# Hand-listed events around three layer norms: the turns that a front does not read go behind the second half's sums

## Chip, cores, metric

The kernel runs on one NeuronCore of a Trainium2 chip. The metric is the device time of one execution in microseconds, the median of several runs. Beside it stands one profiled execution, with times of every instruction.

## What is computed

The reference is one decoder layer on 256 tokens of width 2048, in float32:

```python
h = layer_norm(alpha * h + 0.5 * swiglu(h, w_ffn1_gu, w_ffn1_down))          # norm 0
rq, rk, rv, rg, aq, ak, av, gate_r, gate_a = split(h @ w_in)
mixed = (sigmoid(gate_r) * ret_branch + sigmoid(gate_a) * att_branch) @ w_mix_out
h = layer_norm(alpha * h + mixed)                                            # norm 1
h = layer_norm(alpha * h + 0.5 * swiglu(h, w_ffn2_gu, w_ffn2_down))          # norm 2
ple = sigmoid(h @ w_ple_gate) * (p @ w_ple_proj)
h = layer_norm(alpha * h + ple)                                              # norm 3
```

`swiglu` has an inner width of 5632; `ret_branch` is a chunkwise retention with eight heads, `att_branch` a sliding-window attention with sixteen. The change touches what stands around norms 0, 1 and 2, in the text called the first, the second and the third norm.

## The kernel before

**Weights.** Weights come in chunks of 512 KB. SP issues the loads (line 105, tiles `r...`), ACT makes the high part of each chunk (line 91, tiles `h...`), the DVE the low part (line 92, tiles `l...`), and PE multiplies three times for each product: low by high, high by high, high by low (lines 291 to 293). A list `plan` holds the chunks in the order of use. `fill` takes from it: it loads a chunk while there is room and the queued work is under a limit `far`, and makes a loaded one while the made work is under a limit `ahead` and `room["quiet"]` is not set. `take` hands the next made chunk to the matmuls, `done` gives its slots back and calls `fill`. All instructions are written in one order (the scheduler is told to keep it), so each engine runs its own in that order, and an instruction that waits holds up those behind it on its engine.

**The tokens.** The 256 tokens are two halves of 128 rows, t=0 and t=1. A row half has sixteen blocks of 128 columns. A norm needs the whole row, and the matmuls behind it need the rows turned: features in partitions. So around each norm stand:

- *The held-out steps* (`held_out`): the last chunks before the norm. Their products for t=0 come first, then those for t=1, so that the norm of t=0 runs beside the second half of these matmuls.
- *Sums* (`Norm.normal(t)`): the last block of columns is added to the rows on the DVE (line 891, in the mixers 1280), its statistics are taken (line 530), the reciprocal root of the variance is computed in small DVE instructions, and the first four column blocks are normed (lines 501 and 502).
- *Turns* (`Norm.turn(t, c)`, c = 0 to 3), each four column blocks: the DVE norms the rows of the next turn (`more`), PE transposes (line 509, tile `lnps`; for c=0 two pairs, otherwise four at once), ACT and DVE make high and low part of the result (`ht`, lines 91 and 92). In the second norm ACT also copies two turns into tiles `keep`.
- *The blocks put by* (`put_by`; first and second norm): products of the embedding input `pt` with a small weight, 12 matmuls for each of two blocks, into banks `pp`. ACT copies them to `pps` behind all other events of that stretch, and SP stores them.
- *The front* (`Norm.first`): the first six steps behind the norm (a step is six matmuls of one chunk with one row half), first all six for t=0, then all six for t=1. They read column blocks 0 to 11 in the first and the third norm, thus turns c = 0 to 2; in the second norm 0 to 5, thus turns c = 0 and 1. After the front the steps go on with all columns.

In the held-out stretch n counts half steps of t=1 and on through the blocks put by; in the front n counts steps, 1 to 6 for t=0 and 7 to 12 for t=1. A tuple of such n says when the next event of a fixed list comes:

```python
at, self.at = self.at, self.at + 1
if at == 4:
    self.normal(1)
else:
    self.turn(at // 5, at % 5)
if at == 8:
    quiet(False)
```

So the events are always (0,0), (0,1), (0,2), (0,3), the sums of t=1, (1,0), (1,1), (1,2), (1,3), and behind the last of them making of chunks is allowed again ("go"). It is forbidden (`quiet(j >= len(steps) - 2)`) from the last two held-out steps of t=0 on.

For the three norms these are the places: the first norm has (8, 10, 11, 12, 12) in the held-out stretch and (4, 6, 7, 8) in the front; the second has the same; the third has (8, 11) and then (1, 3, 3, 6, 7, 9, 10).

Of the kernel before, what the change touches and what calls it, by code (L numbers as in the profile page):

```python
# [48 lines left out]
def layer(ctx: ExitStack, tc: tile.TileContext, io):  # L49
# [134 lines left out]
    def fill(must=False):  # L184

        while True:
            queued = sum(u.time for u in ready)
            left = room["slots"] - room["used"]
            wanted = must and not ready or not room["quiet"] and queued < room["ahead"]
            if loaded and wanted and loaded[0].makes <= left:  # L190
                u = loaded.pop(0)
                u.make()
                room["used"] += u.keeps - u.loads
                ready.append(u)
                continue
            first = loaded[0] if loaded else plan[0] if plan else None
            queued += sum(u.time for u in loaded)
            if plan and queued < room["far"] and plan[0].loads + first.makes <= left:
                u = plan.pop(0)
                u.load()  # L200
                room["used"] += u.loads
                loaded.append(u)
                continue
            return

    def take(key):
        if not ready:
# [12 lines left out]
    def quiet(on):  # L220
        room["quiet"] = on
# [197 lines left out]
            done(u)  # L419
            run_side()  # L420

    def held_out(steps, lhs, sums, of_columns, first_done, between, calm=True):

        kept = []
        for j, (key, k0, n) in enumerate(steps):
            u = take(key)
            kept.append(u)
            tokens_chunk(u.chunk, k0, lhs, [sums[t][n] for t in range(2)], (0,))  # L430
            if calm:
                room["ahead"] -= u.time
                room["far"] -= u.time
                quiet(j >= len(steps) - 2)
            fill()
            run_side()
            of_columns(0, j)
        first_done()
        for j, (key, k0, n) in enumerate(steps):
            for kk in range(2):  # L440
                tokens_chunk(kept[j].chunk, k0, lhs, [sums[t][n] for t in range(2)], (1,), (kk,))
                between(2 * j + kk + 1)
            done(kept[j])
            of_columns(1, j)
# [72 lines left out]
    class Norm:  # L517
# [32 lines left out]
            else:  # L550
                ln_turn(*args, 4 * c, 4, self.keep.get(c))

        def follow(self, n, times):


            while times and times[0] == n:
                times.pop(0)
                at, self.at = self.at, self.at + 1
                if at == 4:
                    self.normal(1)  # L560
                else:
                    self.turn(at // 5, at % 5)
                if at == 8:
                    quiet(False)

        def run(self, steps, lhs, times, blks=()):


            self.vectors = vectors.pop()
            self.new = big.tile([P, KD, 512], F32R, tag="ht", name=f"ht{self.i}")  # L570
            per = len(steps) // len(self.cols)
            self.at, times = 0, list(times)
# [5 lines left out]
            held_out(steps, lhs, self.sums, of_columns, lambda: self.normal(0), lambda n: self.follow(n, times))  # L578
            if blks:
                put_by(blks, lambda n: self.follow(2 * len(steps) + n, times))  # L580
            assert not times
# [6 lines left out]
        def first(self, steps, lhs, sums, times):  # L588


            kept, times = [], list(times)
            for j, (key, k0, n) in enumerate(steps):
                u = take(key)
                kept.append(u)
                tokens_chunk(u.chunk, k0, lhs, [sums[t][n] for t in range(2)], (0,))
                fill()
                self.follow(j + 1, times)
            for j, (key, k0, n) in enumerate(steps):
                tokens_chunk(kept[j].chunk, k0, lhs, [sums[t][n] for t in range(2)], (1,))
                done(kept[j])  # L600
                self.follow(len(steps) + j + 1, times)
            assert self.at == 9
            self.put_away()

    def block_stats(stats, y, col):
# [140 lines left out]
    def ffn(name, i, ht, norm, keep, residual, keepers, away):  # L746
# [28 lines left out]
        for j in range(KF // 4):  # L775
            pg, pu = banks(f"{name}g{j}"), banks(f"{name}u{j}")
            units = gu_units(j)
            plain = len(units) - sum(kind == "S" for kind, p in units)
            n_of = {(0, 0): KD, (0, 1): KD, (1, 0): KD, (1, 1): KD}
            for kind, p in units:  # L780
                if kind == "S":
                    for at in ((0, 0), (0, 1), (1, 0)):
                        n_of[at] -= 1
                    n_of[1, 1] -= 2
            sums = [[Sum((pg, pu)[n][t], n_of[t, n]) for n in range(2)] for t in range(2)]
            got = []

            if norm is not None and j == 0:
                front, units = units[:FRONT_PAIRS], units[FRONT_PAIRS:]
                steps = [(gu_keys(name, 0)(n, p), 2 * p, n) for _, p in front for n in range(2)]  # L790
                norm.first(steps, rhs, sums, (4, 6, 7, 8))
                slots_for_weights(24)

            def before(u, j=j, offset=KD // 2 - len(units)):
                u += offset
                if j == 0 and norm is None and u % 2 == 0:
                    first_chunk(u // 2)
                    if u == 6:
# [12 lines left out]
            if got:  # L811
                g, v = got
                for x, ps in ((g, pg), (v, pu)):
                    for t in range(2):
                        dve.tensor_tensor(x[:, t], x[:, t], ps[t], ALU.add)  # L815
                act.activation(g, g, AF.Silu)  # L816
                dve.tensor_tensor(v, g, v, ALU.mult)
            else:
                v = slot([P, 2, 512], F32, f"{name}v{j}")
                for t in range(2):  # L820
                    act.activation(v[:, t], pg[t], AF.Silu)
                for t in range(2):
                    dve.tensor_tensor(v[:, t], v[:, t], pu[t], ALU.mult)
            later(2, lambda j=j, v=v: turned(j, v))
# [50 lines left out]
        def before_unit(u):  # L875
# [4 lines left out]
                load_for_norm(i)  # L880
            if u == len(second) - 1:
                make_for_norm()

        pt_ = [banks(f"{name}e{t}") for t in range(2)]
        sums = [[Sum(pt_[t][n], n_of[1][t, n]) for n in range(2)] for t in range(2)]
# [5 lines left out]
            dve.tensor_tensor(sl, sl, p, ALU.add)  # L891

        norm = Norm((2, 3), sums, combine, y, stats, i, 4 * LN_EPS, keepers, away)
        norm.run(steps, lhs, *(((8, 10, 11, 12, 12), (0, 1)) if i < 2 else ((8, 11),)))
        return norm


# [53 lines left out]
    def mixers(ht, norm, residual, keepers, away):  # L951
# [17 lines left out]

        ps = banks("rv0")  # L970
        sums = [[Sum(ps[t], KD)] for t in range(2)]
        norm.first([(("w_rv", 0, c), 2 * c, 0) for c in range(FRONT)], rhs, sums, (4, 6, 7, 8))
        slots_for_weights(24)
        for c in range(FRONT, KD // 2):
            u = take(("w_rv", 0, c))
# [327 lines left out]
            run_side()  # L1303
        steps = [(("w_mix", 3, c), 2 * c, 0) for c in range(first, KD // 2)]
        norm = Norm((3,), sums, combine, y, stats, 1, LN_EPS, keepers, away)
        norm.run(steps, lhs, (8, 10, 11, 12, 12), (2, 3))
        return norm


    def embedding(ht, norm, y):  # L1310
# [17 lines left out]
        for blk in range(4):  # L1328
# [4 lines left out]
            if blk == 0:  # L1333
                for j in range(4):
                    pp[j] = load_columns(pp, j, "ppr")
                steps = [(key + (c,), 2 * c, 0) for c in range(FRONT)]
                norm.first(steps, lhs, [[s] for s in sums], (1, 3, 3, 6, 7, 9, 10))
                slots_for_weights(24)
                for c in range(FRONT, KD // 2):
                    u = take(key + (c,))  # L1340
# [20 lines left out]
            held_out(steps, lhs, [[s] for s in sums], lambda t, j: None, first_done, lambda n: None, False)  # L1361
            finish(3, pgs[1], sg, 1)
            last_norm(1, *ln_stats(stats[:, 1], 3, 1, LN_EPS))

# [146 lines left out]
```

## Time and profile before

| | |
|---|---|
| time, median of 3 runs | 2303.19 us (2302.16 to 2305.45) |
| the profiled execution: its own time, its span | 2305.66 us, 2303.6 us |
| busy: PE, DVE, ACT | 99%, 84%, 51% of the span |
| PE busy from 400 to 800 us (first norm near 710) | 394.24 of 400 us |
| PE busy from 1200 to 1600 us (second norm near 1490) | 398.48 of 400 us |
| PE busy from 2000 to 2303 us (third norm near 2200, and the end) | 286.01 of 303 us |

Busy time of PE comes from modelled ends of matmuls that overlap: a matmul of 512 columns is shown with some 0.39 us, but the next starts sooner. So the text counts from start to start. An idle time in brackets counts from the shown end of the instruction before.

In a row of the timeline stand the start in us from the span's start, the duration, the engine, the line, the operation, the tile written and the tile read, and in brackets the idle time ahead of it with what ended it. "x2" means that two such instructions were merged. A row of the windows gives from:to, the length, busy time with count for PE, PEld (weight loads), DVE, ACT and POOL, then the granted clock of PE, the DMA share and GB/s.

### The profile page before, as it was taken

What the parts mean: (1) busy time and instruction counts of PE and PEld (TensorE: products, weight loads), DVE (VectorE), ACT (ScalarE), POOL (GpSimd) and SP (SyncE); (2) the same over time, 40 slices, a digit from 0 to 9 for tenths busy, and PEclk for the clock granted to TensorE, in tenths of its full rate; (3) what the DMA queues carried; (4) which work ended last, traced back from release to release, by engine and by line L of the source; (5) the groups of instructions that cost most, each with busy time, mean ns of one, the idle gap of its engine ahead of it and who ended that gap; (6) DMA issues with size and microseconds to landing.
All of it is one profiled execution on the core that took longest, in us unless ns stands there. A gap on an engine that the chain in (4) does not pass through costs nothing.

```text
span 2303.6 us, 28759 instructions
## 1 busy us (share of the span) xinstructions
PE 2271.7 (99%) x10466; PEld 1882.5 (82%) x10466; DVE 1945.0 (84%) x2467; ACT 1184.4 (51%) x1427; POOL 96.0 (4%) x53
## 2 busy tenths in 40 slices
PE   9999999999999999999999999999999999999997
PEld 7788888888887888888778888888888888888876
DVE  7999999988988774677789786779999999889876
ACT  5555555555553342435566454355565565655432
POOL 0000000000000430124000000000000000000000
PEclk9999999999999999999999999999999999999999
DMA  9566666665576665555447567576556566565771
GB/s 317 164 219 192 192 206 195 201 207 182 214 279 237 202 215 169 171 161 163 139 156 236 170 224 274 171 245 206 197 191 203 183 209 215 170 220 193 289 256 56
DMA packets 193725, 465.70 MB, mean 202 GB/s; under 512 B 14768, under 2 KB 16048, under 8 KB 193584
## 3 DMA queue, kind: packets, MB, share of 16 engines
q1 hardware_dynamic: 191456, 460.91, 60.8%
q10 hardware_dynamic: 2128, 2.97, 0.4%
q8 instruction: 82, 1.34, 0.2%
q14 instruction: 59, 0.48, 0.1%
HBM read 455.43 MB, written 8.39 MB: 201 GB/s over the span
## 4 chain that ended last, share of the span: by engine, by line
PE 95%; DVE 3%; DMA 1%; issue 0%; ACT 0%; SPq 0%; ACTq 0%; DVEq 0%
PE f2g L293 3%; PE f2g L291 3%; PE f2g L292 3%; PE f1g L291 3%; PE f1g L292 3%; PE f1g L293 3%; PE rqk L242 3%; PE f2u L292 2%; PE f2u L291 2%; PE f2u L293 2%; PE f1u L291 2%; PE f1u L293 2%; PE f1u L292 2%; PE aqk L242 2%; PE f2d L291 2%; PE f1d L291 2%
## 5 line engine op out<-in xcount | busy, mean ns | idle before, releaser
L92 DVE TENSOR_TENSOR lf_gu<-rf_gu,hf_gu 128x1024 fp32r<-128x1024 f32 (+1 forms) x283 | 334.2, 1213 | 9.6 <-ACT hf_gu L91 9.1
L91 ACT CAST hf_gu<-rf_gu 128x1024 fp32r<-128x1024 f32 (+1 forms) x283 | 282.1, 1045 | 19.4 <-DMA rf_gu<-in_f_gu 19.4
L92 DVE TENSOR_TENSOR lw_in_f<-rw_in_f,hw_in_f 128x1024 fp32r<-128x1024 f32 x140 | 195.6, 1427 | 29.3 <-ACT hw_in_f L91 27.1
L92 DVE TENSOR_TENSOR lf_down<-rf_down,hf_down 128x1024 fp32r<-128x1024 f32 x152 | 180.9, 1219 | 27.5 <-ACT hf_down L91 22.0
L91 ACT CAST hf_down<-rf_down 128x1024 fp32r<-128x1024 f32 x152 | 155.3, 1051 | 77.0 <-DMA rf_down<-in_f_down 27.0
L91 ACT CAST huf_gu<-uf_gu 128x1024 fp32r<-128x1024 f32 x70 | 73.7, 1053 | 159.2 <-DVE uf_gu L164 153.5
L91 ACT CAST hw_in_f<-rw_in_f 128x1024 fp32r<-128x1024 f32 x140 | 138.9, 1051 | 2.3 <-DMA rw_in_f<-in_w_in_f 2.0
L291 PE MATMUL f1g<-hf_gu,xt 128*128 128x512 f32 x247 | 97.2, 393 | 5.4 <-ACT hf_gu L91 5.4
L293 PE MATMUL f1g<-lf_gu,xt 128*128 128x512 f32 x247 | 96.8, 392 | 0.0
L292 PE MATMUL f1g<-hf_gu,xt 128*128 128x512 f32 x247 | 96.8, 392 | 0.0
L291 PE MATMUL f2g<-hf_gu,ht 128*128 128x512 f32 x247 | 96.5, 391 | 0.0
L293 PE MATMUL f2g<-lf_gu,ht 128*128 128x512 f32 x247 | 96.2, 389 | 0.0
L292 PE MATMUL f2g<-hf_gu,ht 128*128 128x512 f32 x247 | 96.1, 389 | 0.0
L91 ACT CAST hvf_gu<-vf_gu 128x1024 fp32r<-128x1024 f32 x70 | 73.8, 1054 | 29.4 <-DVE vf_gu L166 29.4
L816 ACT ACTIVATE eve<-eve 128x1024 f32<-128x1024 f32 x20 | 21.2, 1062 | 127.2 <-DVE eve L815 127.2
L92 DVE TENSOR_TENSOR luf_gu<-uf_gu,huf_gu 128x1024 fp32r<-128x1024 f32 x70 | 85.2, 1218 | 0.0
L92 DVE TENSOR_TENSOR lvf_gu<-vf_gu,hvf_gu 128x1024 fp32r<-128x1024 f32 x70 | 85.2, 1217 | 0.0
L291 PE MATMUL f2u<-hf_gu,ht 128*128 128x512 f32 x212 | 83.5, 394 | 0.0
L291 PE MATMUL f1u<-hf_gu,xt 128*128 128x512 f32 x212 | 83.3, 393 | 0.0
L292 PE MATMUL f2u<-hf_gu,ht 128*128 128x512 f32 x212 | 82.5, 389 | 0.0
L293 PE MATMUL f2u<-lf_gu,ht 128*128 128x512 f32 x212 | 82.5, 389 | 0.0
L292 PE MATMUL f1u<-hf_gu,xt 128*128 128x512 f32 x212 | 82.5, 389 | 0.0
(1333 smaller groups left out, 6433.7 us busy)
## 6 DMA issues: line engine op xcount, KB each, us to landing
rf_gu<-in_f_gu SPq DMA_DIRECT2D x351, 512.0 KB, 5.0
rf_down<-in_f_down SPq DMA_DIRECT2D x176, 512.0 KB, 4.5
rw_in_f<-in_w_in_f SPq DMA_DIRECT2D x148, 512.0 KB, 4.4
rw_rv<-in_w_rv SPq DMA_DIRECT2D x32, 512.0 KB, 4.6
rw_ret<-in_w_ret SPq DMA_DIRECT2D x32, 512.0 KB, 4.7
rw_mix<-in_w_mix SPq DMA_DIRECT2D x32, 512.0 KB, 4.3
rw_pg<-in_w_pg SPq DMA_DIRECT2D x32, 512.0 KB, 4.7
rw_att<-in_w_att SPq DMA_DIRECT2D x16, 512.0 KB, 5.3
```

Of the source, the lines that this page charges most:

```text
L91: act.copy(dst_hi, src)
L92: (lo_engine or dve).tensor_tensor(dst_lo, src, dst_hi, ALU.subtract)
L242: pe.matmul(ps[f], hi[:, kk, f * P : (f + 1) * P], rhs(k), start=k == 0, stop=k == n_k - 1,)
L291: pe.matmul(o, al, bh, start=first, stop=False)
L292: pe.matmul(o, ah, bh, start=False, stop=False)
L293: pe.matmul(o, ah, bl, start=False, stop=self.left == 0)
L816: act.activation(g, g, AF.Silu)
```

## The change

Each norm now gets a written list of events, each with its place n and with what happens: a turn (t, c), "sums" (the sums of t=1), "make" (one more chunk is made, whatever `quiet` says) or "go" (making is allowed again).

- First norm: making is forbidden sooner, from the last unit ahead of the held-out steps on, and `held_out` gets calm=4, so all four of its first-half steps are quiet. With that the fifth and sixth chunk of the front (`rv_4`, `rv_5`) are not made ahead of the sums of t=0 but by two events "make" behind turn (0,2), ahead of the sums of t=1. Turn (0,3) goes from the end of the held-out stretch into the front, behind turn (1,2).
- Second norm: turns (0,2) and (0,3) go into the front, (0,2) between (1,1) and (1,2), (0,3) between (1,2) and (1,3); the sums of t=1 come behind (0,1). (1,0) comes at n=3 and not 4.
- Third norm: turn (0,3) goes from n=3 to n=8, between (1,1) and (1,2); the sums of t=1 come at n=1 and not at n=3.
- "go" comes at n=10 in all three; in the first two norms it was at n=8, in the third at n=10.

Every engine issues the same instructions as before; SP's list has the same order too.

```diff
+    def make_next():
+        u = loaded.pop(0)
+        assert u.makes <= room["slots"] - room["used"]
+        u.make()
+        room["used"] += u.keeps - u.loads
+        ready.append(u)
...
-    def held_out(steps, lhs, sums, of_columns, first_done, between, calm=True):
+    def held_out(steps, lhs, sums, of_columns, first_done, between, calm=2):
...
-                quiet(j >= len(steps) - 2)
+                quiet(j >= len(steps) - calm)
...
-        def follow(self, n, times):
-            while times and times[0] == n:
-                times.pop(0)
-                at, self.at = self.at, self.at + 1
-                if at == 4:
+        def follow(self, n, events):
+            while events and events[0][0] == n:
+                what = events.pop(0)[1]
+                if what == "sums":
                     self.normal(1)
+                elif what == "make":
+                    make_next()
+                elif what == "go":
+                    quiet(False)
                 else:
-                    self.turn(at // 5, at % 5)
-                if at == 8:
-                    quiet(False)
+                    self.turned.append(what)
+                    self.turn(*what)
...
@@ ffn: the front of the second norm
-                norm.first(steps, rhs, sums, (4, 6, 7, 8))
+                norm.first(steps, rhs, sums, (
+                    (3, (1, 0)), (5, (1, 1)), (7, (0, 2)), (8, (1, 2)), (9, (0, 3)), (10, (1, 3)), (10, "go"),
+                ))
...
@@ ffn: ahead of the held-out steps
             if u == len(second) - 1:
                 make_for_norm()
+                quiet(i < 2)
...
@@ ffn: the held-out stretch of the first (i < 2) and the third norm
-        norm.run(steps, lhs, *(((8, 10, 11, 12, 12), (0, 1)) if i < 2 else ((8, 11),)))
+        if i < 2:
+            events = ((8, (0, 0)), (10, (0, 1)), (11, (0, 2)), (12, "make"), (12, "make"), (12, "sums"))
+            norm.run(steps, lhs, events, (0, 1), 4)
+        else:
+            norm.run(steps, lhs, ((8, (0, 0)), (11, (0, 1))))
...
@@ mixers: the front of the first norm
-        norm.first([(("w_rv", 0, c), 2 * c, 0) for c in range(FRONT)], rhs, sums, (4, 6, 7, 8))
+        norm.first([(("w_rv", 0, c), 2 * c, 0) for c in range(FRONT)], rhs, sums, (
+            (5, (1, 0)), (6, (1, 1)), (8, (1, 2)), (9, (0, 3)), (10, (1, 3)), (10, "go"),
+        ))
...
@@ mixers: the held-out stretch of the second norm
-        norm.run(steps, lhs, (8, 10, 11, 12, 12), (2, 3))
+        norm.run(steps, lhs, ((8, (0, 0)), (10, (0, 1)), (10, "sums")), (2, 3))
...
@@ embedding: the front of the third norm
-                norm.first(steps, lhs, [[s] for s in sums], (1, 3, 3, 6, 7, 9, 10))
+                norm.first(steps, lhs, [[s] for s in sums], (
+                    (1, (0, 2)), (1, "sums"), (6, (1, 0)), (7, (1, 1)), (8, (0, 3)), (9, (1, 2)),
+                    (10, (1, 3)), (10, "go"),
+                ))
```

More of the change, by code (lines that the diff above doesn't have):

```diff
@@ L551, in turn, with run @@
                 ln_turn(*args, 4 * c, 4, self.keep.get(c))
-        def follow(self, n, times):
-            while times and times[0] == n:
-                times.pop(0)
-                at, self.at = self.at, self.at + 1
-                if at == 4:
+        def follow(self, n, events):
+            while events and events[0][0] == n:
+                what = events.pop(0)[1]
+                if what == "sums":
                     self.normal(1)
-                else:
-                    self.turn(at // 5, at % 5)
-                if at == 8:
-                    quiet(False)
-        def run(self, steps, lhs, times, blks=()):
+                elif what == "make":
+                    make_next()
+                elif what == "go":
+                    quiet(False)
+                else:
+                    self.turned.append(what)
+                    self.turn(*what)
+        def run(self, steps, lhs, events, blks=(), calm=2):
             self.vectors = vectors.pop()
@@ L571, in run @@
             per = len(steps) // len(self.cols)
-            self.at, times = 0, list(times)
+            self.turned, events = [], list(events)
             def of_columns(t, j):
@@ L576, in of_columns @@
                     self.columns(t, j // per)
-            held_out(steps, lhs, self.sums, of_columns, lambda: self.normal(0), lambda n: self.follow(n, times))
+            held_out(steps, lhs, self.sums, of_columns, lambda: self.normal(0), lambda n: self.follow(n, events), calm)
             if blks:
-                put_by(blks, lambda n: self.follow(2 * len(steps) + n, times))
-            assert not times
+                put_by(blks, lambda n: self.follow(2 * len(steps) + n, events))
+            assert not events
         def put_away(self):
@@ L586, in put_away, with first @@
                     sync.dma_start(self.away[c], self.y[c])
-        def first(self, steps, lhs, sums, times):
-            kept, times = [], list(times)
+        def first(self, steps, lhs, sums, events):
+            kept, events = [], list(events)
             for j, (key, k0, n) in enumerate(steps):
@@ L596, in first @@
                 fill()
-                self.follow(j + 1, times)
+                self.follow(j + 1, events)
             for j, (key, k0, n) in enumerate(steps):
@@ L600, in first @@
                 done(kept[j])
-                self.follow(len(steps) + j + 1, times)
-            assert self.at == 9
+                self.follow(len(steps) + j + 1, events)
+            assert not events and len(set(self.turned)) == 8
             self.put_away()
@@ L1360, in embedding @@
             steps = [(key + (c,), 2 * c, 0) for c in range(KD // 2)]
-            held_out(steps, lhs, [[s] for s in sums], lambda t, j: None, first_done, lambda n: None, False)
+            held_out(steps, lhs, [[s] for s in sums], lambda t, j: None, first_done, lambda n: None, 0)
             finish(3, pgs[1], sg, 1)
```

## The prediction

> **What bounds the kernel now.** I read the page first, then the waits of PE, then the timeline of PE, DVE and SP around the three norms, and the granted clock in short windows there.
>
> ```profile
> PE 2271.7 (99%) x10466; PEld 1882.5 (82%) x10466; DVE 1945.0 (84%) x2467; ACT 1184.4 (51%) x1427; POOL 96.0 (4%) x53
> ```
> PE is busy for all but 32 us of the span of 2303.6 us. The change adds and removes no instruction, so only what PE loses between matmuls can be won. The waits of PE (total, times, longest) say where:
>
> ```profile
> PE lnps L509 <- DVE f1y L502: 5.3, 3, 4.8
> PE lnps L509 <- DVE f2y L502: 2.4, 3, 1.6
> PE lnps L509 <- DVE mixy L502: 1.2, 3, 0.5
> ```
> Apart from the start, the end and some single microseconds, PE waits at the turns (the transposes, `lnps`) of the three norms, and for the DVE, which makes the rows that PE turns. The first norm carries the longest wait. PE there, start and duration first:
>
> ```profile
> 706.00 0.39 PE L293 MATMUL f1e<-lf_down,f1ah 128*128 128x512 f32 x1
> 711.15 0.66 PE L509 MATMUL lnps<-ident,f1y 128*128 128x128 f32 x2 [4.77 <-DVE f1y L502]
> 711.98 0.69 PE L509 MATMUL lnps<-ident,f1y 128*128 128x128 f32 x2 [0.17 <-DVE f1y L502]
> ...
> 728.01 0.41 PE L509 MATMUL lnps<-ident,f1y 128*128 128x128 f32 x2 [0.51 <-ACT ht L91]
> ...
> 732.83 0.60 PE L509 MATMUL lnps<-ident,f1y 128*128 128x128 f32 x4
> ...
> 734.66 0.60 PE L509 MATMUL lnps<-ident,f1y 128*128 128x128 f32 x4
> ...
> 740.57 0.39 PE L291 MATMUL rv<-hw_rv,ht 128*128 128x512 f32 x1
> ```
> At 706.00 PE starts its last matmul of the second sums (the second row half, t=1); the next event is the first transpose at 711.15. The idle also has a tail:
>
> ```profile
> 710.00:715.00 5.00, 3.68 (x10) 2.76 (x11) 4.86 (x11) 0.75 (x2) 0.00 (x0) 0.50 0.03 13
> ```
> The granted clock (the column after POOL) is 0.50 just after the gap. So the gap costs its 4.77 us and some slow matmuls. Two units are read from these rows. A turn and a step of six matmuls together take 734.66 - 732.83 = 1.83 us; from 734.66 a turn and four steps take 740.57 - 734.66 = 5.91 us; so a **step is 1.36 us** and a **turn 0.47 us**. 740.57 is the first matmul behind the front, the mark by which I count this norm.
>
> Why the DVE is late is in its own timeline:
>
> ```profile
> 699.43 0.68 DVE L92 TENSOR_TENSOR pt<-praw,pt 128x512 fp32r<-128x512 f32 x1
> 702.85 2.53 DVE L92 TENSOR_TENSOR lw_rv<-rw_rv,hw_rv 128x1024 fp32r<-128x1024 f32 x2 [2.73 <-ACT hw_rv L91]
> 705.30 0.68 DVE L891 TENSOR_TENSOR f1y<-f1y,f1e 128x512 f32<-128x512 f32 x1
> ...
> 711.44 0.48 DVE L502 SCALAR_TENSOR_TENSOR f1y<-f1y,rstd,ln_b 128x256 f32<-128x256 f32 x1
> ...
> 713.93 0.75 DVE L502 SCALAR_TENSOR_TENSOR f1y<-f1y,rstd,ln_b 128x512 f32<-128x512 f32 x1
> 714.60 0.75 DVE L92 TENSOR_TENSOR ht<-lnps,ht 128x256 fp32r<-128x256 f32 x2
> ...
> 722.55 0.68 DVE L891 TENSOR_TENSOR f1y<-f1y,f1e 128x512 f32<-128x512 f32 x1
> ...
> 736.86 2.36 DVE L92 TENSOR_TENSOR lw_rv<-rw_rv,hw_rv 128x1024 fp32r<-128x1024 f32 x2 [0.26 <-ACT hw_rv L91]
> ```
> The split of `pt` ends at 700.1. Then the DVE stands 2.73 us, waiting for ACT casts of two weight chunks, splits them (702.85), and only at 705.30 adds the first sums to the rows. These sums were there earlier: the 24 matmuls of the second half precede 706.23, so the first half ended at about 706.23 - 4 x 1.36 = 700.8, its first column block 2.7 us before.
>
> **First norm, part by part.** The two chunk splits go behind the turns (0,0) to (0,2), so the DVE adds the first sums at 700.1 instead of 705.30, 5.2 us sooner; the second block is wanted 1.3 us later, when it is there. PE's transposes of (0,0) at 711.15 and 711.98 could start at 705.95 and 706.8. PE is free at 706.23: the first does not wait, the second waits 0.4 us. Then follow 24 matmuls (5.44 us) and the turns (0,1) and (0,2) without (0,3), 0.94 us; with 0.2 for the pair itself the front starts at 706.8 + 6.6 = 713.4. The rows for (0,1), ready at 714.68 before (713.93 + 0.75), come at 709.5 and are wanted at 709.7: covered, barely. No gap of 4.8 us is left, so the half clock goes too.
>
> What is late next is the second norm, because the two chunk splits stand ahead of its sums. From 709.5 the DVE has the two small splits of the first turn (714.60, 0.75 together), four row operations of 0.75, two splits of the shape of `pt`'s, 0.68 each, and the two chunk splits, 2.53 together: 7.6 us by durations, 7.1 start to start (2.53 from 702.85 overlaps the next start at 705.30 by 0.08, as do its neighbours). The second sums are added at 716.6 instead of 722.55. Behind them only this norm's own work waits. The second transposes of (1,0) move by the same 5.95 us from 728.01 to 722.06. PE comes there at 713.4 + 5 steps = 720.2 and loses about 1.5 us in two pieces. Then seven steps and four turns ((1,1), (1,2), (0,3), (1,3)) are left: 0.2 + 9.52 + 1.88 = 11.6, which ends the front at 733.6 instead of 740.57: **7.0 us less**. The chunk splits moved are needed at PE's fifth step, 718.8, and done at 716.6.
>
> The turn (0,3) itself costs the same 0.47 us later, as its rows are read only behind the front. The release ("go") of further chunks comes two steps nearer to the front's end. From the last turn at 734.66 to the first chunk split behind it (736.86 plus half of 2.36) are 3.4 us; PE now needs it 0.47 + 2 x 1.36 + 0.45 (two matmuls that don't read it) = 3.6 us after that turn. This holds by 0.2 us; without it each of three norms loses what the split is late.
>
> On ACT, the two casts now stand ahead of the four copies of `pps`, and SP stands at the stores behind these:
>
> ```profile
> 722.91 1.30 SPq L650 DMA_DIRECT2D ppd<-pps  x2
> ```
> ```profile
> L91 ACT CAST hw_in_f<-rw_in_f 128x1024 fp32r<-128x1024 f32 x140 | 138.9, 1051 | 2.3 <-DMA rw_in_f<-in_w_in_f 2.0
> ...
> rw_in_f<-in_w_in_f SPq DMA_DIRECT2D x148, 512.0 KB, 4.4
> ```
> Nothing moved issues a DMA, but the chunks behind these stores on SP wait with them. Turn (0,2) is on PE near 711.8 and cast by 713; two casts of 1.05 us (the row is that of an equal chunk) end near 715, and the four copies follow. Even with 4 us for those, SP goes on at 719 and not at 722.91. The raw tiles of the two chunks come free at 716.6 instead of 705.4, still ahead of that. I cost both at nothing, since PE's need of the chunks behind the stores starts near 739.
>
> **Second norm.** Two turns, (0,2) and (0,3), leave the stretch ahead of the second sums:
>
> ```profile
> 1489.07 0.69 DVE L92 TENSOR_TENSOR ht<-keep,ht 128x512 fp32r<-128x512 f32 x1 [1.27 <-ACT ht L91]
> ...
> 1493.21 0.68 DVE L1280 SCALAR_TENSOR_TENSOR mixy<-mixy,mo 128x512 f32<-128x512 f32 x1
> ```
> The DVE can add them where the split at 1489.07 ends, 1489.7, not at 1493.21: 3.5 us sooner. PE:
>
> ```profile
> 1497.75 0.41 PE L509 MATMUL lnps<-ident,mixy 128*128 128x128 f32 x2 [0.32 <-DVE mixy L502]
> 1498.67 0.41 PE L509 MATMUL lnps<-ident,mixy 128*128 128x128 f32 x2 [0.51 <-DVE mixy L502]
> ...
> 1511.83 0.39 PE L291 MATMUL f2g<-hf_gu,ht 128*128 128x512 f32 x1
> ```
> The second transposes of (1,0), now after step three, come at 1495.15. PE was through step four at 1497.4 (1497.75 less its idle 0.32); with one step and two turns less it is there by 1495.1, so nothing else is late. Nine steps, five turns and 0.2 are left, 14.8 us, and the mark 1511.83 becomes 1509.9: **1.9 us less**. The sums' early place delays only turns whose readers come later.
>
> **Third norm.** Here the second sums go from behind (0,3), event three, to event one:
>
> ```profile
> 2195.89 0.68 DVE L92 TENSOR_TENSOR ht<-lnps,ht 128x512 fp32r<-128x512 f32 x1
> ...
> 2199.51 0.68 DVE L891 TENSOR_TENSOR f2y<-f2y,f2e 128x512 f32<-128x512 f32 x1
> ...
> 2206.18 0.74 DVE L92 TENSOR_TENSOR ht<-lnps,ht 128x256 fp32r<-128x256 f32 x2
> ```
> The row splits end at 2196.5, so the sums move from 2199.51 by 3.0 us. PE:
>
> ```profile
> 2201.96 0.39 PE L293 MATMUL pg<-lw_pg,ht 128*128 128x512 f32 x1
> 2203.96 0.44 PE L509 MATMUL lnps<-ident,f2y 128*128 128x128 f32 x2 [1.61 <-DVE f2y L502]
> 2204.96 0.66 PE L509 MATMUL lnps<-ident,f2y 128*128 128x128 f32 x2 [0.57 <-DVE f2y L502]
> 2206.66 0.79 PE L291 MATMUL pg<-hw_pg,ht 128*128 128x512 f32 x1 [1.03 <-DVE ht L92]
> ...
> 2218.58 0.39 PE L291 MATMUL pg<-hw_pg,ht 128*128 128x512 f32 x1
> ```
> PE, less one turn, is at (1,0) at 2202.2 - 0.47 = 2201.7; the transposes come at 2201.0 and 2202.0, and the second half's first matmul, which waits for the first of the splits at 2206.18, at 2203.7 instead of 2206.66. So the waits 1.61 + 0.57 + 1.03 shrink to about 1.5. Six steps and four turns follow, 10.05 us at full clock: the mark 2218.58 becomes 2213.7, **4.9 us less**. Of these 2.3 are not the wait but the clock: before, six steps and three turns took 11.92 instead of 9.6 us, at
>
> ```profile
> 2205.00:2210.00 5.00, 3.97 (x11) 2.88 (x12) 3.31 (x6) 0.37 (x1) 0.00 (x0) 0.50 0.33 105
> ```
> This is the disputed term. The clock fell after 3.2 us of waits, of which none was over 1.61. It did not fall at the second norm, where 0.32 and 0.51 us stood together:
>
> ```profile
> 1495.00:1500.00 5.00, 4.18 (x20) 3.07 (x19) 4.65 (x15) 1.56 (x4) 0.00 (x0) 1.00 1.00 340
> ```
> The 1.5 us that I leave lies between the two. I take the clock to hold, since the fall had twice as much idle in one window, and keep the other end for the range.
>
> The Trainium skill ("TensorE: Matmul & The Clock Gate", section "What's actually happening") states that the clock halves after at least one idle window of about 3.4 us; by that no gap under 3.4 us would count, and the third norm's pieces should not have tripped it. The trace disagrees: 0.50 after pieces of 1.61, 0.57 and 1.03. So the measurement decides: a share of idle is enough, and how large a share is open. By the page's rule alone my 1.5 us gaps would be harmless and the forecast the sum below; by the row of 0.50 the rival below keeps its chance.
>
> **The sum.** 7.0 + 1.9 + 4.9 = 13.8 us, from waits and half clock removed. Against the profiled execution (span 2303.6, its own time 2305.66, so 2.1 us lie around the span) that is 2291.9; the shown median, 2303.19, is 2.5 us under the profiled one, and from it I take the same 13.8: 2289.4, said as **2289.5 us**.
>
> **The rivals.**
> *Half clock left over.* The 1.5 us waits at (1,0) of the first or the third norm halve the clock again. Price 2.3 us each: 2291.8 with one, 2294.1 with both. For it: the fall at the third norm without a long gap. Against: the waits are half as much as then.
>
> *The splits were not the cause.* If in another run the chunk ahead of `pt` lands later, the DVE starts the sums late anyway, each us past 700.4 costs one, up to the 5 us of before; norms two and three keep their gain. About 2294.5. Against: the DVE's row at 699.43 has no wait ahead of it, and the rows say the sums were done. The new order itself is sure: the engines' program of the changed kernel has exactly these moves.
>
> *Slower: the feature weights run dry.* SP stands behind the `pps` stores. If their copies, behind two casts more on ACT, came late, PE would run out of chunks in the stage behind the first norm. PE wants the third such chunk near 739 + 5.6 = 744.8; with 4.4 us to landing (the row above) and some 2 us to make it, it must be issued by 738; SP gets there near 719. Each us past 738 is a us lost, so slower from 738 + 13.8 = 752 on: 2305 needs SP free at 754, 31 us later than the 722.91 of before. Nothing in the rows points there.
>
> *No change.* The waits move to (1,0) in full and the clock falls as often: 2303. Against: PE's arrival there is counted above; only 1.5 us remain.
>
> **How the numbers follow.** Forecast 0.52; half clock once or twice 0.32; late data 0.09; no change 0.04; slower 0.03. 0.2%, about 4.6 us, is what a measurement can tell here. The first three are all over it: faster 0.93, same 0.04, slower 0.03. Range: below, up to 3 us of the 1.5 us waits may vanish where DVE operations overlap more than I count: 2286.5. Above, both half clocks, 2294.1, and the spread of the runs before (2302.16 to 2305.45) on top: 2296.5.
>
> **What would show it.** In the new profile the row additions of the first norm start within 1 us of the end of `pt`'s split; the first transposes of the first norm follow the last second-sum matmul with under 1 us; PE's waits at the turns total under 5 us instead of 8.9; fronts end 7.0, 1.9 and 4.9 us sooner relative to the last first-sum matmul; no window at the first norm has a clock of 0.50. The forecast is wrong if the DVE still waits ahead of the sums, if the (1,0) waits are over 2 us, or if a chunk behind a front is waited for by over 0.5 us.

## The result, and the profile after

The changed kernel took 2292.70 us (median of 5 runs, 2292.15 to 2293.51), the kernel before, run beside it, 2304.34 us (5 runs, 2302.16 to 2306.40). The ratio is 0.995 with a 95% interval of 0.9935 to 0.9964: **faster by 11.6 us, 0.5%**. The forecast was 2289.5 us, 3.2 us too low, inside its range of 2286.5 to 2296.5. The span of the profiled execution fell from 2303.6 to 2290.8 us, by 12.8 us.

The line of busy time of the changed kernel's page:

```profile
PE 2266.2 (99%) x10466; PEld 1879.6 (82%) x10466; DVE 1945.5 (85%) x2467; ACT 1183.6 (52%) x1427; POOL 95.8 (4%) x53
```
The work is the same, yet PE is busy 5.5 us less. In the main that part is not waiting: it is matmuls that ran at the clock of 0.50 before. (Part of it may come from the modelled ends, since a matmul ahead of a wait is shown with its full length.) The rest, 7.3 us, is idle time that went. The waits of PE (total, times, longest), start and end of the kernel left out:

```profile
PE pg L298 <- DVE ht L92: 1.3, 1, 1.3
...
PE lnps L516 <- DVE f1y L509: 1.0, 2, 0.5
PE lnps L516 <- DVE f2y L509: 0.7, 2, 0.4
...
PE lnps L516 <- DVE mixy L509: 0.3, 1, 0.3
```
Line numbers are higher here than before: the transposes are line 516 (509 before), the row operations 509 (502), the sums 904 (891). At the turns 2.0 us are left of 8.9. The first wait is that for the split at the third norm. PE's timeline at the first norm:

```profile
706.26 0.39 PE L300 MATMUL f1e<-lf_down,f1ah 128*128 128x512 f32 x1
706.49 0.77 PE L516 MATMUL lnps<-ident,f1y 128*128 128x128 f32 x4
...
721.02 0.41 PE L516 MATMUL lnps<-ident,f1y 128*128 128x128 f32 x2 [0.48 <-DVE f1y L509]
721.94 0.41 PE L516 MATMUL lnps<-ident,f1y 128*128 128x128 f32 x2 [0.51 <-DVE f1y L509]
...
733.65 0.39 PE L298 MATMUL rv<-hw_rv,ht 128*128 128x512 f32 x1
```
The first transposes follow directly the last matmul of the held-out steps for t=1; the gap of 4.77 us is gone. The two pieces at (1,0) lie at 721.02 and 721.94. The first matmul behind the front comes at 733.65, where it came at 740.57. The DVE's timeline of the same stretch:

```profile
699.54 0.68 DVE L92 TENSOR_TENSOR pt<-praw,pt 128x512 fp32r<-128x512 f32 x1
700.14 0.68 DVE L904 TENSOR_TENSOR f1y<-f1y,f1e 128x512 f32<-128x512 f32 x1
...
714.22 2.35 DVE L92 TENSOR_TENSOR lw_rv<-rw_rv,hw_rv 128x1024 fp32r<-128x1024 f32 x2
716.48 0.68 DVE L904 TENSOR_TENSOR f1y<-f1y,f1e 128x512 f32<-128x512 f32 x1
...
732.65 2.36 DVE L92 TENSOR_TENSOR lw_rv<-rw_rv,hw_rv 128x1024 fp32r<-128x1024 f32 x2 [0.26 <-ACT hw_rv L91]
```
Nothing stands between the split of `pt` and the first sums any more; the two chunk splits lie at 714.22, ahead of the second sums. At the second norm one wait is left, 0.33 us, and PE's first matmul behind that front is now

```profile
1503.18 0.39 PE L298 MATMUL f2g<-hf_gu,ht 128*128 128x512 f32 x1
```
where it was at 1511.83. The windows of the changed kernel at the first and the third norm:

```profile
705.00:710.00 5.00, 5.00 (x26) 3.92 (x25) 4.86 (x10) 0.74 (x2) 0.00 (x0) 1.00 0.09 37
710.00:715.00 5.00, 5.00 (x28) 4.07 (x27) 4.93 (x8) 3.19 (x5) 0.00 (x0) 1.00 0.01 3
...
2190.00:2195.00 5.00, 4.28 (x21) 3.32 (x20) 4.61 (x15) 0.65 (x2) 0.00 (x0) 1.00 0.72 285
2195.00:2200.00 5.00, 4.43 (x23) 3.71 (x24) 2.95 (x6) 1.07 (x2) 0.00 (x0) 1.00 0.67 185
```
The clock stays at 1.00 at both. The third norm on PE:

```profile
2181.04 0.44 PE L516 MATMUL lnps<-ident,f2y 128*128 128x128 f32 x2 [0.42 <-DVE f2y L509]
2183.81 0.66 PE L516 MATMUL lnps<-ident,f2y 128*128 128x128 f32 x4 [0.24 <-DVE f2y L509]
...
2193.68 0.60 PE L516 MATMUL lnps<-ident,f2y 128*128 128x128 f32 x4
2195.57 0.50 PE L298 MATMUL pg<-hw_pg,ht 128*128 128x512 f32 x1 [1.29 <-DVE ht L92]
...
2205.78 0.39 PE L298 MATMUL pg<-hw_pg,ht 128*128 128x512 f32 x1
```
The transposes of (1,0) at 2193.68 wait for nothing; of 1.61, 0.57 and 1.03 us one wait of 1.29 is left. By the marks (the first matmul behind each front) the three norms gave 740.57 - 733.65 = 6.9, then 1.7 (1511.83 became 1503.18, 8.65 in all) and 4.15 us (2218.58 became 2205.78, 12.80 in all).

### The profile page after: what moved, and what is told of

Its sections match the earlier page's. It is cut to its first block, busy times and chain, and to the rows that moved or that the text cites. A ratio compares the mean times of both kernels' runs of the same rounds, so it can differ in the third digit from the quotient of the medians.

```text
span 2290.8 us, 28764 instructions
## 1 busy us (share of the span) xinstructions
PE 2266.2 (99%) x10466; PEld 1879.6 (82%) x10466; DVE 1945.5 (85%) x2467; ACT 1183.6 (52%) x1427; POOL 95.8 (4%) x53
## 3 DMA queue, kind: packets, MB, share of 16 engines
q8 instruction: 82, 1.34, 0.2%
## 4 chain that ended last, share of the span: by engine, by line
PE 96%; DVE 3%; DMA 1%; issue 0%; ACT 0%; SPq 0%; ACTq 0%; DVEq 0%
PE f1g L298 3%; PE f1g L299 3%; PE f1g L300 3%; PE f2g L298 3%; PE f2g L300 3%; PE f2g L299 3%; PE rqk L249 3%; PE f1u L299 2%; PE f1u L300 2%; PE f1u L298 2%; PE f2u L298 2%; PE f2u L299 2%; PE f2u L300 2%; PE aqk L249 2%; PE f1d L300 2%; PE f2d L299 2%
```

## The experiments

Theory: the DVE came late to three places, each norm's wait is its own, and the clock falls after a share of idle. Rivals: the gains hang together (DMA order, clock); the place of the turns and not the chunk splits did it; only a long gap slows the clock. In all, the kernel before ran at medians of 2304.57 us beside the first four, 2303.55 beside the next four and 2303.93 beside the last three.

A "slow step" below is a stretch of 3.41 us at the clock of 0.50; experiment 1 shows that length.

**1. One norm at a time** (three kernels; the other two norms keep the lists of before). The list of the second, undone in the first and the third of them:

```diff
-        norm.run(steps, lhs, ((8, (0, 0)), (10, (0, 1)), (10, "sums")), (2, 3))
+        norm.run(steps, lhs, ((8, (0, 0)), (10, (0, 1)), (11, (0, 2)), (12, (0, 3)), (12, "sums")), (2, 3))
```


> First norm as in the changed kernel, second and third norms as before. If the three gains are separate and additive: about 6.9 us under the kernel before, by span near 2296.7; the third norm keeps its waits of 1.6, 0.6 and 1.0 us and a stretch of half clock, the first has none. If the first norm's gain were given back later: within 2 us of before.

> Second norm alone as in the changed kernel. By my count in the prediction 1.9 us under the kernel before, by the rows of the changed kernel 1.6 (span near 2302). Rival: the gain there came only because the first norm had shifted the DMAs: no difference. Half clock at the first and the third norm as before.

> Third norm alone as in the changed kernel. Additive: 4.3 us less by the rows of the changed kernel (4.9 in the prediction), of which 2.3 is the half clock that goes; span near 2299.3. Rival: the clock holds at the third norm only because nothing had slowed it at the first; then it falls again and the gain is about 2.

| changed | median, us | under before | ratio, 95% interval |
|---|---|---|---|
| first norm only | 2298.72 | 5.85 | 0.9967 to 0.9984 |
| second only | 2302.70 | 1.87 | 0.9983 to 1.0001 |
| third only | 2299.66 | 4.91 | 0.9970 to 0.9988 |

They add up to 12.6 us, against 11.6 for all three; the difference is well inside the intervals. So the gains are separate as far as these times can tell, and none is seen to be given back later. The first norm alone measured 5.85 us, where 6.9 was expected; its interval reaches from 3.7 to 7.6. The second alone is not told from nothing by its times; its trace has one wait of 0.3 where before stood three of 1.2. With the third norm alone the clock holds there although it fell at the first. With the first alone, the third norm has the waits of before, yet the clock was low for half as long as before:

```profile
2193.85:2197.26 3.41, 1.80 (x9) 1.07 (x7) 3.05 (x13) 0.00 (x0) 0.00 (x0) 1.00 0.24 95
2197.26:2200.67 3.41, 1.56 (x8) 1.09 (x8) 3.32 (x7) 0.74 (x2) 0.00 (x0) 1.00 0.11 40
2200.68:2204.09 3.41, 3.41 (x12) 2.72 (x11) 1.57 (x3) 0.59 (x1) 0.00 (x0) 0.50 0.79 217
2204.09:2207.50 3.41, 3.41 (x19) 2.80 (x17) 1.52 (x3) 0.59 (x1) 0.00 (x0) 1.00 0.86 321
```
These are windows cut where the clock changes. In this case's profiles every stretch at 0.50 ahead of the kernel's end lasts 3.41 or 6.83 us: one such step here, two at the same place of the kernel before:

```profile
2201.15:2204.56 3.41, 1.64 (x8) 0.86 (x6) 3.06 (x13) 0.13 (x1) 0.00 (x0) 1.00 0.36 144
2204.56:2207.97 3.41, 1.97 (x5) 1.41 (x6) 3.34 (x7) 0.61 (x2) 0.00 (x0) 0.50 0.19 44
2207.98:2211.39 3.41, 3.41 (x11) 2.72 (x11) 0.69 (x2) 0.59 (x1) 0.00 (x0) 0.50 0.67 190
2211.39:2214.80 3.41, 3.41 (x18) 2.79 (x18) 1.80 (x3) 0.58 (x1) 0.00 (x0) 1.00 0.99 358
```
Nearly the same waits (1.61, 0.57 and 1.28 us here, 1.61, 0.57 and 1.03 there) thus cost one or two slow steps. Where they fall against these steps differs: here 1.61 us of idle lie in the first step (3.41 - 1.80) and 1.85 in the second, there 1.77 in the first.

**2. Turns moved, chunks not held back.**

```diff
-                quiet(i < 2)
...
-            events = ((8, (0, 0)), (10, (0, 1)), (11, (0, 2)), (12, "make"), (12, "make"), (12, "sums"))
-            norm.run(steps, lhs, events, (0, 1), 4)
+            events = ((8, (0, 0)), (10, (0, 1)), (11, (0, 2)), (12, "sums"))
+            norm.run(steps, lhs, events, (0, 1))
```


> The changed kernel, but at the first norm the two front chunks are made ready ahead of the first sums, as before; the turns keep their new places. If the two chunk splits were the cause: the gap of about 4.8 us and the half clock at the first norm are back, and of that norm's 6.9 us only about 1.5 stay (one split of 0.68 less ahead of the second sums and turns moved): some 5.4 us over the changed kernel, 7.4 under the kernel before. If the turns' places did it: as the changed kernel. If the data was late for another reason: the gap stays away.

Measured: 2297.49 us, 7.1 under the kernel before (interval 0.9960 to 0.9983) and 4.8 over the changed kernel. The DVE and PE of that run:

```profile
699.37 0.69 DVE L92 TENSOR_TENSOR pt<-praw,pt 128x512 fp32r<-128x512 f32 x1
699.97 1.22 DVE L92 TENSOR_TENSOR lw_rv<-rw_rv,hw_rv 128x1024 fp32r<-128x1024 f32 x1
702.28 1.23 DVE L92 TENSOR_TENSOR lw_rv<-rw_rv,hw_rv 128x1024 fp32r<-128x1024 f32 x1 [1.09 <-PE f1e L299]
703.42 0.68 DVE L903 TENSOR_TENSOR f1y<-f1y,f1e 128x512 f32<-128x512 f32 x1
```
```profile
709.28 0.41 PE L516 MATMUL lnps<-ident,f1y 128*128 128x128 f32 x2 [2.79 <-DVE f1y L509]
710.10 0.68 PE L516 MATMUL lnps<-ident,f1y 128*128 128x128 f32 x2 [0.42 <-DVE f1y L509]
```
The splits ahead of the first sums, with what they wait for, bring the gap back (and the clock falls for one step): shown. The gap is 2.8 and not 4.8 us in this execution, because the first chunk was there earlier than in the profile of before (its split starts at 699.97, not after a wait of 2.73); the second split still waited 1.09 us, by the row for a matmul of PE. In the three profiles with the first norm's order of before (the kernel before, second only, third only) the wait ahead of the two splits was 2.73, 2.54 and 2.20 us, and the ACT cast ahead of them waited 2.98, 2.80 and 2.46 us for its transfer. So how late the DVE is there changes from execution to execution with the landing of a transfer. The changed order removes that dependence: in all nine profiles with the chunks held back the first sums follow the split of `pt` directly. The turns alone are worth about 2.1 of this norm's 6.9 us (6.9 - 4.8).

**3. Chunks held back, turn (0,3) back ahead of the second sums.**

```diff
-            events = ((8, (0, 0)), (10, (0, 1)), (11, (0, 2)), (12, "make"), (12, "make"), (12, "sums"))
+            events = ((8, (0, 0)), (10, (0, 1)), (11, (0, 2)), (12, (0, 3)), (12, "make"), (12, "make"), (12, "sums"))
...
-            (5, (1, 0)), (6, (1, 1)), (8, (1, 2)), (9, (0, 3)), (10, (1, 3)), (10, "go"),
+            (4, (1, 0)), (6, (1, 1)), (7, (1, 2)), (8, (1, 3)), (8, "go"),
```


> The changed kernel, but at the first norm turn (0,3) stands ahead of the second sums again and the front's events are those of before; the two chunks stay held back. The first gap stays away. The second sums come about 0.7 us later and PE arrives earlier at (1,0), after four steps: waits there of about 2.6 us instead of 1.0. Time 1.4 us over the changed kernel if the clock holds, 3.7 over it if such waits halve the clock. If the move of the turn was worth nothing: no difference.

Measured: 2296.58 us, 3.9 over the changed kernel: the case with the half clock. PE waits at (1,0) for 2.94 and 0.51 us, and the clock falls for one step:

```profile
722.96 0.41 PE L516 MATMUL lnps<-ident,f1y 128*128 128x128 f32 x2 [2.94 <-DVE f1y L509]
```
```profile
723.54:726.95 3.41, 3.07 (x9) 2.52 (x10) 3.34 (x7) 0.61 (x2) 0.00 (x0) 0.50 1.01 408
```
Without something for PE to do while the chunks are split, much of the gap only moves from the first to the second sums: holding the chunks back alone is worth about 3.0 of the 6.9 us at this norm. The other 3.9 need the turn's new place. This edit also puts the front's other events and the "go" back, so the turn's place is not parted from those. The two halves of the change, alone 2.1 and 3.0 us, give less than 6.9 together. Each alone leaves one slow step, and only both leave none; that the missing 1.8 us are this step is not shown, but they are near its price in experiment 4.

**4. One more chunk split ahead of the third norm's second sums.**

```diff
-                    (1, (0, 2)), (1, "sums"), (6, (1, 0)), (7, (1, 1)), (8, (0, 3)), (9, (1, 2)),
+                    (1, (0, 2)), (1, "make"), (1, "sums"), (6, (1, 0)), (7, (1, 1)), (8, (0, 3)), (9, (1, 2)),
```


> The changed kernel with one more chunk split (1.2 us on the DVE) ahead of the second sums of the third norm: PE's waits there rise from 1.3 us to about 2.5 us in pieces of at most 1.5. If the clock falls by the share of idle and the limit lies under 2.5 us: 1.2 + 2.3 = 3.5 us over the changed kernel, with a stretch of 0.50. If the limit lies over it, or if only a gap of some 3.4 us counts: 1.2 us over it and no such stretch. If the DVE is not what is late there: no difference.

Measured: 2294.79 us, 2.1 over the changed kernel (2.4 over its second measurement, below); the span of the profiled execution is 2.7 over. PE's timeline, then the windows:

```profile
2193.98 0.44 PE L516 MATMUL lnps<-ident,f2y 128*128 128x128 f32 x2 [0.36 <-DVE f2y L509]
2194.89 0.44 PE L516 MATMUL lnps<-ident,f2y 128*128 128x128 f32 x2 [0.48 <-DVE f2y L509]
2196.68 0.50 PE L298 MATMUL pg<-hw_pg,ht 128*128 128x512 f32 x1 [1.34 <-DVE ht L92]
```
```profile
2194.41:2197.82 3.41, 1.59 (x8) 1.17 (x8) 3.34 (x7) 0.74 (x2) 0.00 (x0) 1.00 0.38 111
2197.82:2201.23 3.41, 3.41 (x12) 2.72 (x11) 1.27 (x2) 0.59 (x1) 0.00 (x0) 0.50 0.88 220
2201.24:2204.65 3.41, 3.41 (x20) 2.85 (x20) 1.78 (x3) 1.17 (x2) 0.00 (x0) 1.00 0.87 291
```
The idle in brackets grew by 0.9 us, from 1.29 to 2.18. From start to start the split costs its whole length: from turn (0,2) to the first matmul of t=1 PE takes 2196.68 - 2186.18 = 10.50 us here and 2195.57 - 2186.38 = 9.19 in the changed kernel, 1.3 more. And the clock fell for one step after pieces of at most 1.34 us, of which 1.82 us lie in the step ahead (3.41 - 1.59). From that matmul to the mark PE takes 2208.49 - 2196.68 = 11.81 us, in the changed kernel 2205.78 - 2195.57 = 10.21: one slow step full of matmuls costs 1.6 us. Together that is 2.9; turn (0,2) came 0.2 us sooner in this execution, hence the 2.7 of the span. I had expected 3.5, with the price of the two slow steps of before. The DVE is what is late there, and the limit lies under 1.82 us of idle in a step.

**5. What is still late.** Four orders were run against the waits that the changed kernel keeps. In the first, turn (1,0) does its splits ahead of the next turn's row operations, in all norms:

```diff
-            if c < 3:
+            if c < 3 and (t, c) != (1, 0):
                 self.more(t, c + 1)
...
                     ln_turn(*args, k0, 2, self.keep.get(c))
+                if t:
+                    self.more(t, 1)
```


> The changed kernel, but in turn (1,0) of each norm the DVE does the splits of the turned rows before the row operations (1.5 us) of the next turn. The wait of 1.3 us for the first split at the third norm shrinks to about 0.6, the rows of (1,1) come 0.7 us later, which PE reaches two steps later at the earliest: 0.5 to 0.7 us under the changed kernel. Rival: the rows of (1,1) are then what is late and the time stays.

Measured: 2293.76 us, 1.1 over the changed kernel, where 0.5 to 0.7 under it was expected. The third norm does as expected (1.3 became 0.7 us, 0.2 came back at the next turn). At the first norm the rival's wait is there, and the time rises instead of staying: (1,1) comes one step behind (1,0), not two as I had written, and PE, which had not waited for the splits there, now waits for the rows:

```profile
724.30 0.63 PE L516 MATMUL lnps<-ident,f1y 128*128 128x128 f32 x4 [1.08 <-DVE f1y L509]
```
In the second, the first norm's second sums go ahead of both held chunks; in the third, between them:

```diff
-            events = ((8, (0, 0)), (10, (0, 1)), (11, (0, 2)), (12, "make"), (12, "make"), (12, "sums"))
+            events = ((8, (0, 0)), (10, (0, 1)), (11, (0, 2)), (12, "sums"), (12, "make"), (12, "make"))   # second
+            events = ((8, (0, 0)), (10, (0, 1)), (11, (0, 2)), (12, "make"), (12, "sums"), (12, "make"))   # third
```


> The changed kernel, but at the first norm the second sums stand ahead of the two held chunks. The waits at (1,0) (1.0 us) go, but the splits of the two chunks end at about 720.6 and 721.8, and PE wants the first at 718.8: a wait of about 1.4 to 2 us on a chunk takes its place, so 0.5 to 1 us over the changed kernel. Rival: PE's need of the chunks is later than I count, and the time falls by 1.0.

> The changed kernel, but at the first norm the second sums stand between the two held chunks. The sums come 1.2 us sooner, so the two waits at (1,0) (1.0 us) go; the first chunk is there in time and the second is split at about 721.8, 0 to 0.5 us after PE wants its low part: 0.5 to 1.0 us under the changed kernel. Rival: PE waits for the second chunk in full, and the wait has only moved once more: no difference.

Measured: 2292.97 us with both chunks behind the sums, the same as the changed kernel (0.5 to 1 us over it was expected, from a wait of 1.4 to 2): the waits at (1,0) are gone and one of 1.07 us on the chunk has taken their place.

```profile
720.14 0.50 PE L300 MATMUL rv<-lw_rv,ht 128*128 128x512 f32 x1 [1.07 <-DVE lw_rv L92]
```
With the sums between the two: 2291.76 us, 0.6 under the changed kernel beside it (2292.38); PE waits there for 0.17 and 0.26 us instead of 1.0. The fourth adds the first order at the third norm alone:

> The same, and at the third norm alone the splits of turn (1,0) stand ahead of the row operations of the next turn: the wait of 1.3 us for the first split falls to 0.7, 0.2 of it comes back at the next turn. Another 0.4 us under the kernel before this one, in all 0.9 to 1.4 under the changed kernel.

> The changed kernel itself, beside the two others on the same chip: 11 to 12.5 us under the kernel before; no stretch of half clock at the norms.

Measured, side by side on one chip (5 runs each): 2291.53 us (2291.15 to 2292.26), the changed kernel 2292.38 (2291.90 to 2292.96). So the best order found is 0.85 us under the changed kernel, about as much as the five runs of either spread, and 12.4 under the kernel before (interval 0.9932 to 0.9957). That the fourth order is better than the third is not shown: it is 0.2 us under it, where 0.4 was expected.

## Why the prediction was right, and where its number was off

- *First norm, 7.0 us.* The mark moved by 6.92. Each step came as worked out: first sums at 700.14 (700.1 predicted), second sums at 716.48 (716.6), second transposes of (1,0) at 721.94 (722.06), waits there 1.0 us (1.5), mark 733.65 (733.6). What was thinner than it looked is the data: in three of the nine profiles with the chunks held back the second block of the first sums waited 0.18 to 0.32 us for PE. The slack of 0.2 us at the chunk behind the front held: its first split ends at 732.65 + 1.2 = 733.85 and PE wants it at 733.65 + 0.45 = 734.1.
- *Second norm, 1.9 us.* 1.7 by the marks. The 1.9 by the medians with this norm alone is no proof, since its interval reaches from a small loss to 3.9 us.
- *Third norm, 4.9 us.* 4.15 by the marks. The (1,0) part came, with 1.29 us of waits instead of 1.5. What the sum left out is ahead of it: PE waited 0.42 us at (0,0), where the profile before has no wait, since the DVE reached the first sums later against PE. (The 0.24 at (0,1) stood there before as well, with 0.25.) That is over half of the 0.75 us that are missing. The DVE's last splits ahead of those sums, in the changed kernel and in the kernel before:

```profile
2171.95 2.49 DVE L92 TENSOR_TENSOR lw_pg<-rw_pg,hw_pg 128x1024 fp32r<-128x1024 f32 x2 [0.74 <-ACT hw_pg L91]
```
```profile
2181.28 1.22 DVE L92 TENSOR_TENSOR lw_pg<-rw_pg,hw_pg 128x1024 fp32r<-128x1024 f32 x1 [0.15 <-ACT hw_pg L91]
```
  The splits waited 0.74 instead of 0.15 us for ACT's casts, and these for landings. In the second profile of the changed kernel the waits of PE at the third norm's transposes are

```profile
PE lnps L516 <- DVE f2y L509: 0.2, 1, 0.2
```
  and there is none at (0,0). On the other hand the profiles "first norm only" and "second only", which have the third norm's old list, wait 0.33 and 0.35 us at (0,0). So this wait goes with the execution more than with the list; the profile that the sum was made from happened to have none.
- *The clock, the disputed term.* It held at both places, as I took it, but not for the reason that I gave. I had read that it fell after 3.2 us of waits. The windows of experiment 1 show that it fell at 2204.56, after a step with 1.77 us of idle: the wait of 1.61 and the start of the next. The rest of the 0.57 and the whole 1.03 came when the clock was already down. At the norms the runs put the limit between 1.61 us of idle in a step of 3.41 (the clock stayed) and 1.77 (it fell). So the 1.5 us that I counted lay not at half of the idle that trips it but a few tenths of a us under it, and that the forecast came through there is in part luck. The waits left are 0.99 and 1.29 us in all, so in these executions the rival "half clock left over" could not come in, wherever the steps lie; experiment 4, with 1.82 in one step, is over the limit.
- *The rule of the Trainium skill.* "TensorE: Matmul & The Clock Gate" in the Trainium skill, section "What's actually happening", was followed in its length of a window, about 3.4 us: the steps are 3.41 us. But a window does not have to be idle: 1.77 us of idle in it were enough.
- *Late data, slower, no change.* None came. In the first profile of the changed kernel the split of `pt` was not held up, the `pps` stores left SP at 715.89, and no feature chunk was waited for. (In the working of that rival 739 + 5.6 is 744.6, not 744.8; nothing hangs on it.) But the landing of the chunks does vary, and with the splits ahead of the sums the gap varies with it (4.77, 4.7, 4.2 and 2.8 us in four profiles).
- *From the sum to the number: the step that was off.* The sum of 13.8 us was right to 1 us for the execution it was made from: 2305.66 - 13.8 = 2291.9, and the changed kernel took 2292.7. I then took the same 13.8 from the median of three runs, 2303.19. So of the 3.3 us between 2289.4 and 2292.7 the sum accounts for 0.8 and the base for 2.5. The median of three was low (five runs gave 2304.34, later medians were 2303.55 to 2304.57), and the profile was a long execution: of 47 further executions of the kernel before, seven took longer. It had two slow steps at both the first and the third norm, four in all, where the profiles with the first or the third norm left as before had one or two at each. The times of the 47 go with their mean granted clock, which one slow step lowers by 0.0007: the eleven at 0.995, as in the profile, took 2305.4 us on average, the 35 at 0.996 took 2304.0, the one at 0.997 took 2301.5. The changed kernel has no slow step at the norms, and its five runs spread over 1.4 us where those of before spread over 4.2. The waits and slow steps of one long execution can't be taken from the time of a shorter one that has fewer of them.

## What to carry to other kernels

Where a late engine stands ahead of a norm, list what lies on it between the last sum and the first row that PE wants, and move out what nobody reads yet; then count the next place where the same engine is late, because without the turn and the front's events moved as well (experiment 3) more than half the gain would have been lost there. Where waits of one to two microseconds stand close together, add them up per 3.41 us: in this kernel up to 1.61 us between matmuls cost what they lasted, and 1.77 or more cost one or two slow steps on top. Take a gain that comes out of a profile from the time of that same execution, above all where the thing removed varies from run to run.

## What the runs showed of the hardware

In these profiles the granted clock changes only at steps of 3.41 us, and whether it does goes with PE's idle in the step before. At the norms, full-speed steps with 1.77, 1.82, 1.85 us of idle or more were followed by one at 0.50; one with 1.61 was not. The end of the kernel, where PE runs out of work, narrows this: steps with 1.71 us ("third only") and 1.73 us (the first order of experiment 5) were followed by another step at 1.00. So by the shown busy time the limit lies between 1.73 and 1.77 us, a little over half of a step; the ends of matmuls are modelled, so an exact share is not shown, nor whether the transposes, which stand in the steps at the norms and not in those at the end, count like other matmuls. The pieces themselves were never over 1.61 us at the third norm.

At 0.50 the clock stayed low after steps with 1.07 to 1.78 us of idle and came back after steps with 0.34 or less; nothing between was seen. At 0.50 each matmul of 512 columns takes longer (0.43 instead of 0.23 us from start to start), so a limit read at full speed does not hold there as it stands.

A slow step full of matmuls cost 1.6 us (experiment 4); one with waits in it costs less, as the two at the third norm before, 2.3 us together. Waits of 2.2 to 5 us in a cluster cost one slow step or two, by where they fall, which is one source of the spread of the kernel before.
